# Where activation operands are rounded in a Strassen-staged layer, and two additions handed to accumulating DMAs

## The chip, the cores and the metric

One core of one Trainium2 chip runs the whole program. The metric is the device time of one execution in microseconds (us). Engines are called TensorE (PE in the rows, PEld for its weight loads), VectorE (DVE), ScalarE (ACT), GpSimd (POOL) and SyncE (SP, which here only issues DMAs).

## The reference, cut to what matters

The reference is one transformer-like layer for 640 token rows (512 of a prompt, 8 x 16 of a decode batch), with a model width of 2048. After the mixers (attention and a state-space group), which the change leaves alone, it computes

```python
h = x + merged @ w_out                                    # 2048 x 2048
f = rms_norm(h, g_ffn)
h = h + (silu(f @ w_gate) * (f @ w_up)) @ w_down          # 2048 x 5632, 5632 x 2048
gate = sigmoid(rms_norm(h, g_ple) @ w_ple_gate)           # 2048 x 2048
h = h + gate * (p_i @ w_ple_proj)
```

in float32. The three `h = ... + ...` are the additions that this document is about.

## The kernel before, in words

Features lie on the 128 partitions and the 640 tokens along the free axis. The five big products are done by one level of Strassen-Winograd: a tile of the output is 256 features x 640 tokens, held as `r` (128 x 2 x 640), and seven products of 128 x 320 each take the seven of the eight PSUM banks. The inner dimension goes in *units* of 512 rows. For each unit the `Ring` loads a 512 KB block of weights (`wst`, two buffers), VectorE makes four sums of its quadrants (`ws`, L109 to L112), ScalarE rounds quadrants and sums to a short format (`wh`, L86, once 128 x 768 from `wst` and once 128 x 1024 from `ws`) and VectorE takes what is left (`wl`, L87). The activations are held the same way as high and low parts in `kp` tiles of 2 x 7 x 320 (`cut`, L1050 on ScalarE and L1051 on VectorE; `whole` cuts all seven pieces). So each unit is 7 products x 2 halves x 3 = 42 matmuls of 128x128 on 128x320.

`strassen` runs a tile's units, then combines the seven banks into `r` (L1232 to L1240: two copies on ScalarE, six additions on VectorE, the last one, of `r12`, on GpSimd). The stages, in order:

- `o0` to `o7`: `w_out`, 4 units each, operand `km`. Then the residual `x` is added (L1280), the sum is scaled (`scaled`, L1267, ScalarE), the Winograd sums of its quadrants are written to `fc_dr`, `r` to `h_dr`, and its squares are added up (`squares`, L1249 to L1254: the square on ScalarE, the sums on VectorE).
- `g0`, `u0` to `g21`, `u21`: gate and up, 4 units each, operand `kf`, fetched from `fc_dr` during `o7`.
- `d0` to `d27`: the down product in 28 *cells* of 2 to 4 units (`down_cells`), operand `kt`. All but the last cell of each of the eight output tiles add their part to `h_dr` by an accumulating DMA from the GpSimd queue (L1346). The eight last cells (`d20` to `d27`, output tiles 4 to 7 and 0 to 3, 3 units each) add what `h_dr` holds (L1349, L1350), and go on as the `o` tiles do.
- `p0` to `p7`: the per-layer gate, 4 units each, operand `kh`. The gate is multiplied by a projection `pj`, then the running sum is loaded again (`hy`, L1372), added by GpSimd (L1373) and written out (L1374).

`pair` gives `r`, `x`, `hx`, `pj` and `hy` out of one pool with two buffers, `seven` the scaled tiles (one buffer). Each engine and each DMA queue works its instructions off in order, and that order is made by a scheduler that runs over the whole program when it is built: code that is written later in Python is not always later on the engine, and a moved call changes the order elsewhere. A second `x` tile is also the scratch for the squares.

Of the kernel before, what the change touches and what calls it, by code (L numbers as in the profile page):

```python
# [9 lines left out]
F32 = mybir.dt.float32  # L10
# [4 lines left out]
OP = mybir.AluOpType  # L15
# [4 lines left out]
P = 128  # L20
D = 2048
KT = D // P
NTOK = 640
# [141 lines left out]
def hybrid_step(ctx: ExitStack, tc: tile.TileContext, io):  # L165
    nc = tc.nc
# [5 lines left out]
    dp = ctx.enter_context(tc.tile_pool(reuse_waits="tile", name="dram", bufs=1, space=DRAM))  # L172
# [17 lines left out]
    ring = Ring(nc, stp, units)  # L190
# [4 lines left out]
    g_dr = dp.tile([1024, NTOK], F32, name="g_dr")  # L195
    m_dr = dp.tile([D, NTOK], F32, name="m_dr")
    h_dr = dp.tile([D, NTOK], F32, name="h_dr")
    h2_dr = dp.tile([D, NTOK], F32, name="h2_dr")
    tc_dr = dp.tile([FT // 2, P, 7, NH2], F32, name="tc_dr")
    fc_dr = dp.tile([KT // 2, P, 7, NH2], F32, name="fc_dr")  # L200
    hc_dr = dp.tile([KT // 2, P, 7, NH2], F32, name="hc_dr")
# [844 lines left out]
    def rows(dram, j):  # L1046
        return dram[2 * j * P : 2 * (j + 1) * P, :].rearrange("(a p) n -> p a n", p=P)
# [31 lines left out]
    for n in range(8):  # L1079
        ps = big(f"glu{n}")  # L1080
        g = gp_.tile([P, NTOK], F32, tag="xg", name=f"gre{n}", bufs=3)
# [61 lines left out]
    def pair(name):  # L1143
        return fo.tile([P, 2, NTOK], F32, tag="R", name=name, bufs=2)
# [12 lines left out]
    def kp_tile(name, i):  # L1157
        if i < 5:
            return kp_view(act_tile(name))
        if i == 5:  # L1160
            return fo.tile([P, 2, 7, NH2], F32R, tag="kp", name=name, bufs=1)
        return xp.tile([P, 2, 7, NH2], F32R, tag="kp", name=name, bufs=KB)

    def seven(name):
        return xp.tile([P, 7, NH2], F32, tag="c7", name=name, bufs=1)
# [6 lines left out]
    def whole(k, x):  # L1172
        cut(k, slice(0, 4), x[:, :4])
        cut(k, slice(4, 7), x[:, 4:])
        return k

    later = {}

    def fetch(name, slot, dram, i, late=False):
        k = kp_tile("k" + name, slot)  # L1180
        x = k[:, 1].bitcast(F32)
        nc.sync.dma_start(x, dram[i])
        if late:
            later.setdefault(i // 2 - 2, []).append(lambda: whole(k, x))
            return k
        return whole(k, x)

    def cut_late(u):
        for f in later.pop(u, ()):
            with tc.issue_after(ring.done[0]), tc.issue_after(ring.done[1]):  # L1190
                f()

    def products(name, kps, after=None, order=None):

        ps = {i: bank(f"{name}_{i}")[:, :NH2] for i in PRODUCTS}
        n = len(kps) // 2

        def product(i, u, cut):
            a, b = PRODUCTS[i]
            wh, wl = cut  # L1200
            for c in range(2):
                w = slice(c * P, (c + 1) * P)
                k = kps[2 * u + c]
                f, l = u == 0 and c == 0, u == n - 1 and c == 1
                nc.tensor.matmul(ps[i], wh[:, a, w], k[:, 0, b], start=f, stop=False)  # L1205
                nc.tensor.matmul(ps[i], wh[:, a, w], k[:, 1, b], start=False, stop=False)  # L1206
                nc.tensor.matmul(ps[i], wl[:, a, w], k[:, 0, b], start=False, stop=l)  # L1207

        for u in range(n if order is None else n - 2):
            cut = ring.next()  # L1210
            for i in PRODUCTS:
                product(i, u, cut)
            if after is not None:
                after(u)
        if order is not None:
            cuts = [ring.next() for _ in range(2)]
            for i in order:
                for u in range(2):
                    product(i, n - 2 + u, cuts[u])
        ring.ahead()  # L1220
        return ps
# [4 lines left out]
    def strassen(name, kps, after=None, into=None):  # L1226
        ps = products(name, kps, after)
        r = pair("r" + name) if into is None else into
        r11, r12, r21, r22 = blocks(r)
        q = fo.tile([P, NH2], F32, tag="q", name="q" + name, bufs=1)  # L1230
        tt = nc.vector.tensor_tensor
        nc.scalar.activation(q, ps[1], AF.Copy)  # L1232
        tt(r11, q, ps[2], op=OP.add)
        nc.scalar.activation(r12, ps[3], AF.Copy)
        tt(q, q, ps[6], op=OP.add)
        tt(r22, q, ps[7], op=OP.add)  # L1236
        tt(r12, r12, ps[5], op=OP.add)
        tt(r21, r22, ps[4], op=OP.subtract)
        tt(r22, r22, ps[5], op=OP.add)
        nc.gpsimd.tensor_tensor(r12, r12, q, op=OP.add)  # L1240
        return r
# [14 lines left out]
    def by_rows(x, s):  # L1256
        nc.vector.tensor_tensor(x, x, s[:, None, :].to_broadcast([P, 2, NTOK]), op=OP.mult)  # L1257
# [6 lines left out]
    def scaled(c, x, gain, j):  # L1264

        for a in range(2):
            nc.scalar.activation(c[:, 2 * a : 2 * a + 2], halves(x[:, a]), AF.Copy, scale=gain[:, 2 * j + a : 2 * j + a + 1])  # L1267

    fk = []
    for j in range(8):  # L1270
        after = None
        if j == 7:
            def after(u):
                for i in (2 * u, 2 * u + 1):
                    if i < 7:
                        fk.append(fetch(f"f{i}", i, fc_dr, i, late=i == 6))
        r = strassen(f"o{j}", mk, after)
        x = pair(f"x{j}")
        nc.sync.dma_start(x, io["xT"][2 * j : 2 * j + 2].rearrange("a p n -> p a n"))
        nc.vector.tensor_tensor(r, r, x, op=OP.add)  # L1280
        c = seven(f"c{j}")
        scaled(c, r, gffn, j)
        if j < 7:
            keep(nc.vector, c, fc_dr, j)
        else:
            winograd_rows(nc.vector, c[:, :4], c[:, 4:])
            kf7 = kp_tile("kf7", 7)
            fk.append(kf7)
            later.setdefault(1, []).append(lambda: whole(kf7, c))
        nc.sync.dma_start(rows(h_dr, j), r)  # L1290
        squares(ssqh, r, x, j == 0)

# [2 lines left out]
    def next_t():  # L1295

        u = len(tk) // 2
        if u < FT // 4:
            for i in (2 * u, 2 * u + 1):
                tk[i] = fetch(f"t{i}", slots[i % 8], tc_dr, i)  # L1300

    for f in range(FT // 2):
        z = strassen(f"g{f}", fk, cut_late if f == 0 else None)
        if f == 0:
            scale_rows(ssqh, D)
        by_rows(z, ssqh)
        nc.scalar.activation(z, z, AF.Silu)
        after = None
        if f == FT // 2 - 1:
            def after(u):  # L1310
                if u < 2:
                    next_t()
        c = seven(f"t{f}")
        t = c[:, :4].rearrange("p (a h) n -> p a (h n)", a=2)
        strassen(f"u{f}", fk, after, t)
        by_rows(t, ssqh)
        nc.vector.tensor_tensor(t, t, z, op=OP.mult)
        keep(nc.gpsimd, c, tc_dr, f)
# [12 lines left out]

    for n, (j, us, first, last) in enumerate(cells):
        def after(i, us=us, n=n):
            uses[us[i]] -= 1
            if not uses[us[i]] and n < len(cells) - 4:
                next_t()
            if n < 2 and i:
                next_t()
            if n == len(cells) - 1:
                for _ in range(min(2, 3 - i)):  # L1340
                    if ready:
                        next_h()

        r = strassen(f"d{n}", [tk[i] for u in us for i in (2 * u, 2 * u + 1)], after)
        if not last:
            nc.gpsimd.dma_start(rows(h_dr, j), r, accum_op=OP.add)  # L1346
            continue
        x = pair(f"hx{j}")
        nc.sync.dma_start(x, rows(h_dr, j))  # L1349
        nc.vector.tensor_tensor(r, r, x, op=OP.add)  # L1350
        c = seven(f"hc{j}")
        scaled(c, r, gple, j)
        if j in (3, 4, 5):
            winograd_rows(nc.vector, c[:, :4], c[:, 4:])
            hk[j] = whole(kp_tile(f"kh{j}", hslot[j]), c)
        else:
            keep(nc.vector, c, hc_dr, j)
            ready.append(j)
        nc.sync.dma_start(rows(h2_dr, j), r)
        squares(ssqp, r, x, j == 4)  # L1360
    hk = [hk[i] for i in (4, 5, 6, 7, 0, 1, 2, 3)]
    for j in range(7):
        z = strassen(f"p{j}", hk)
        if j == 0:
            scale_rows(ssqp, D)
        by_rows(z, ssqp)
        nc.scalar.activation(z, z, AF.Sigmoid)  # L1367
        x = pair(f"pj{j}")
        nc.sync.dma_start(x, rows(pj_dr, j))
        nc.vector.tensor_tensor(z, z, x, op=OP.mult)  # L1370
        x = pair(f"hy{j}")
        nc.sync.dma_start(x, rows(h2_dr, j))  # L1372
        nc.gpsimd.tensor_tensor(z, z, x, op=OP.add)  # L1373
        nc.sync.dma_start(rows(io["o_yT"], j), z)  # L1374


    x = pair("pj7")
    y = seven("hy7")[:, :4].rearrange("p (a h) n -> p a (h n)", a=2)
    nc.sync.dma_start(x, rows(pj_dr, 7))
    nc.sync.dma_start(y, rows(h2_dr, 7))  # L1380
    ps = products("p7", hk, order=(1, 2, 6, 5, 3, 7, 4))
    z = pair("rp7")
    r11, r12, r21, r22 = blocks(z)
# [143 lines left out]
```

## Time and profile before

| | |
|---|---|
| median of 3 runs | 2952.66 us (2950.65 to 2954.16) |
| the profiled execution | 2953.62 us, of which the span from first to last instruction is 2951.8 us |
| mean granted TensorE clock | 0.982 |
| busy share of the span: TensorE, VectorE, ScalarE, GpSimd | 96%, 77%, 42%, 14% |

The times of runs and of the profiled execution are of the same kind. The shares are means over stages that differ, so the rows below are taken stage by stage. In the rows, a name such as `ro` is the tile `r` of an `o` stage, `rd` of a `d` stage, `rp` of a `p` stage; buffer numbers are left out.

### The profile page before, as it was taken

Reading aid. Unit: us, or ns where it says so; the run is one execution under the profiler, and the core shown is the slowest. Engines: PE = TensorE matmul, PEld = TensorE weight load, DVE = VectorE, ACT = ScalarE, POOL = GpSimd, SP = SyncE. Lnnn points to the kernel's source line nnn. Section 1 sums busy time; section 2 is a strip of 40 time slices with the busy share of each in tenths; the row PEclk is TensorE's granted clock in tenths of the full one; section 3 lists DMA queues with packets and bytes.
Section 4 is the critical chain, followed back from the end, with each engine's and each line's share of the span. In section 5 each row is a group of like instructions: output and inputs, shape, how many; then the busy total and the mean of one; then the engine's idle time right before and its main releaser. Section 6 shows DMA issues by size and latency. Waiting matters only on the chain. (4 is left out here: it accounts for less than half of the span.)

```text
span 2951.8 us, 47685 instructions
## 1 busy us (share of the span) xinstructions
PE 2827.2 (96%) x19051; PEld 2717.0 (92%) x19051; DVE 2265.6 (77%) x3912; ACT 1240.9 (42%) x1627; POOL 420.7 (14%) x463
## 2 busy tenths in 40 slices
PE   8899999998799989999999999999999999999998
PEld 6789998887789889999999999999989999998898
DVE  8939354455698888787878787878886877899888
ACT  4333365555643453333333333333433444355433
POOL 6612310001000001010101010101020100100111
PEclk9999999999989999999999999999999999999999
DMA  5565744547534633233323333333554445647444
GB/s 168 153 180 159 224 168 173 176 145 260 191 133 172 223 139 123 100 116 101 118 100 118 101 117 102 117 102 117 190 159 139 144 158 175 164 153 271 139 156 143
DMA packets 137487, 449.19 MB, mean 152 GB/s; under 512 B 14096, under 2 KB 34672, under 8 KB 124464
## 3 DMA queue, kind: packets, MB, share of 16 engines
q1 hardware_dynamic: 120032, 396.47, 39.2%
q0 software_dynamic: 15936, 45.47, 6.2%
q10 hardware_dynamic: 1296, 4.20, 0.4%
q8 instruction: 149, 2.44, 0.3%
q14 instruction: 74, 0.61, 0.1%
HBM read 342.25 MB, written 101.18 MB: 150 GB/s over the span
## 5 line engine op out<-in xcount | busy, mean ns | idle before, releaser
L86 ACT ACTIVATE wh<-wst 128x768 fp32r<-128x768 f32 x328 | 276.9, 845 | 659.3 <-issue 319.9
L87 DVE TENSOR_TENSOR wl<-ws,wh 128x1024 fp32r<-128x1024 f32 x328 | 421.0, 1284 | 101.4 <-ACT wh L86 101.0
L86 ACT ACTIVATE wh<-ws 128x1024 fp32r<-128x1024 f32 x328 | 344.6, 1051 | 358.9 <-DVE ws L112 358.9
L87 DVE TENSOR_TENSOR wl<-wst,wh 128x768 fp32r<-128x768 f32 x328 | 337.5, 1029 | 169.3 <-ACT wh L86 169.3
L1205 PE MATMUL d<-kt,wh 128*128 128x320 f32 x1232 | 383.6, 315 | 11.8 <-ACT wh L86 5.1
L1205 PE MATMUL g<-kf,wh 128*128 128x320 f32 x1232 | 381.6, 310 | 5.5 <-ACT wh L86 5.4
L1206 PE MATMUL g<-kf,wh 128*128 128x320 f32 x1232 | 381.1, 310 | 0.0
L1205 PE MATMUL u<-kf,wh 128*128 128x320 f32 x1232 | 380.3, 309 | 0.5 <-DVE rg L1236 0.4
L1206 PE MATMUL d<-kt,wh 128*128 128x320 f32 x1232 | 380.7, 312 | 0.0
L1206 PE MATMUL u<-kf,wh 128*128 128x320 f32 x1232 | 380.1, 309 | 0.0
L1207 PE MATMUL g<-kf,wl 128*128 128x320 f32 x1232 | 375.6, 310 | 4.4 <-DVE wl L87 4.4
L1207 PE MATMUL u<-kf,wl 128*128 128x320 f32 x1232 | 376.1, 309 | 0.6 <-DVE wl L87 0.6
L1207 PE MATMUL d<-kt,wl 128*128 128x320 f32 x1232 | 344.5, 315 | 7.4 <-DVE wl L87 7.3
L1205 PEld LDWEIGHTS d<-kt,wh 128*128 128x128 f32 x1232 | 235.1, 191 | 17.7 <-ACT wh L86 9.7
L1205 PEld LDWEIGHTS g<-kf,wh 128*128 128x128 f32 x1232 | 232.1, 188 | 6.8 <-ACT wh L86 6.8
L1207 PEld LDWEIGHTS g<-kf,wl 128*128 128x128 f32 x1232 | 230.2, 188 | 5.5 <-DVE wl L87 5.2
L1206 PEld LDWEIGHTS d<-kt,wh 128*128 128x128 f32 x1232 | 235.1, 191 | 0.0
L1207 PEld LDWEIGHTS d<-kt,wl 128*128 128x128 f32 x1232 | 224.8, 191 | 11.2 <-DVE wl L87 10.6
L1206 PEld LDWEIGHTS g<-kf,wh 128*128 128x128 f32 x1232 | 232.2, 189 | 0.0
L1205 PEld LDWEIGHTS u<-kf,wh 128*128 128x128 f32 x1232 | 231.2, 188 | 1.0 <-DVE rg L1236 0.7
L1206 PEld LDWEIGHTS u<-kf,wh 128*128 128x128 f32 x1232 | 231.2, 188 | 0.0
L1207 PEld LDWEIGHTS u<-kf,wl 128*128 128x128 f32 x1232 | 230.0, 188 | 0.9 <-DVE wl L87 0.9
(499 smaller groups left out, 5981.2 us busy)
## 6 DMA issues: line engine op xcount, KB each, us to landing
wst<-in_w_gate SPq DMA_DIRECT2D x88, 512.0 KB
wst<-in_w_up SPq DMA_DIRECT2D x88, 512.0 KB
wst<-in_w_down SPq DMA_DIRECT2D x88, 512.0 KB
tc_dr<-t SPq DMA_DIRECT2D x22, 1120.0 KB
kt<-tc_dr SPq DMA_DIRECT2D x22, 1120.0 KB
wst<-in_w_qk SPq DMA_DIRECT2D x32, 512.0 KB
kc<-in_cache_k SPq DMA_DIRECT2D x16, 1024.0 KB
vc<-in_cache_v SPq DMA_DIRECT2D x16, 1024.0 KB
```

Source lines behind the costliest of these rows:

```text
L86: a = nc.scalar.activation(wh[:, part], x, AF.Copy)
L87: b = nc.vector.tensor_tensor(wl[:, part], x, wh[:, part].bitcast(F32), op=OP.subtract)
L1205: nc.tensor.matmul(ps[i], wh[:, a, w], k[:, 0, b], start=f, stop=False)
L1206: nc.tensor.matmul(ps[i], wh[:, a, w], k[:, 1, b], start=False, stop=False)
L1207: nc.tensor.matmul(ps[i], wl[:, a, w], k[:, 0, b], start=False, stop=l)
```

## The change

Three things are edited.

1. *Where operands are rounded.* `fetch` and the two places that called `whole` at once now put the cut into a list (`uncut`). `cut_next` takes the oldest entry of it; it is called after a unit's weights have been asked for, one or two entries at a time. `products` cuts what the coming unit still needs and has not been cut. `cut_late`, which tied two late cuts to the end of a unit's weights, goes.
2. *Residuals.* `residual` adds `x` (for `o0` to `o6`) and the running sum in `h_dr` (for `d20` to `d26`) to `r` by an accumulating DMA on the GpSimd queue, from HBM into `r`. The tile `x` stays as scratch for the squares. For `o7` and `d27` (`urgent`) the load and the VectorE addition stay.
3. *Final addition.* The last `d` cells write their sums to the output `o_yT` itself (only output tile 7 goes to a scratch, `h7_dr`), and the `p` tiles 0 to 6 are added to it by an accumulating DMA on the GpSimd queue; the load of `hy`, the GpSimd addition and the SyncE write go.

`squares` is not edited: its square stays on ScalarE, and its sums were on VectorE before.

```diff
-    h2_dr = dp.tile([D, NTOK], F32, name="h2_dr")
+    h7_dr = dp.tile([2 * P, NTOK], F32, name="h7_dr")
...
-    def fetch(name, slot, dram, i, late=False):
+    uncut = {}
+
+    def wait_cut(k, x):
+        uncut[id(k)] = lambda: whole(k, x)
+        return k
+
+    def fetch(name, slot, dram, i):
         k = kp_tile("k" + name, slot)
         x = k[:, 1].bitcast(F32)
         nc.sync.dma_start(x, dram[i])
...
-        return whole(k, x)
+        return wait_cut(k, x)
+
+    def cut_next(n=1):
+        for key in list(uncut)[:n]:
+            uncut.pop(key)()
...
             cut = ring.next()
+            for k in kps[2 * u : 2 * u + 2]:
+                if id(k) in uncut:
+                    uncut.pop(id(k))()
             for i in PRODUCTS:
                 product(i, u, cut)
...
+    def residual(r, src, name, urgent):
+        x = pair(name)
+        if urgent:
+            nc.sync.dma_start(x, src)
+            nc.vector.tensor_tensor(r, r, x, op=OP.add)
+        else:
+            nc.gpsimd.dma_start(r, src, accum_op=OP.add)
+        return x
...
-                        fk.append(fetch(f"f{i}", i, fc_dr, i, late=i == 6))
+                        fk.append(fetch(f"f{i}", i, fc_dr, i))
+                cut_next((0, 1, 2, 0)[u])
         r = strassen(f"o{j}", mk, after)
-        x = pair(f"x{j}")
-        nc.sync.dma_start(x, io["xT"][2 * j : 2 * j + 2].rearrange("a p n -> p a n"))
-        nc.vector.tensor_tensor(r, r, x, op=OP.add)
+        if j == 7:
+            cut_next()
+        x = residual(r, io["xT"][2 * j : 2 * j + 2].rearrange("a p n -> p a n"), f"x{j}", j == 7)
...
-        z = strassen(f"g{f}", fk, cut_late if f == 0 else None)
+        z = strassen(f"g{f}", fk, (lambda u: cut_next(2)) if f == 0 else None)
...
+                cut_next((0, 1, 1, 0)[u])
...
         strassen(f"u{f}", fk, after, t)
+        cut_next()
...
         def after(i, us=us, n=n):
+            cut_next()
...
-        x = pair(f"hx{j}")
-        nc.sync.dma_start(x, rows(h_dr, j))
-        nc.vector.tensor_tensor(r, r, x, op=OP.add)
+        x = residual(r, rows(h_dr, j), f"hx{j}", j == 3)
...
-            hk[j] = whole(kp_tile(f"kh{j}", hslot[j]), c)
+            hk[j] = wait_cut(kp_tile(f"kh{j}", hslot[j]), c)
...
-        nc.sync.dma_start(rows(h2_dr, j), r)
+        nc.sync.dma_start(rows(io["o_yT"] if j < 7 else h7_dr, j % 7), r)
...
-        z = strassen(f"p{j}", hk)
+        z = strassen(f"p{j}", hk, (lambda u: cut_next(2)) if j == 0 else None)
...
-        x = pair(f"hy{j}")
-        nc.sync.dma_start(x, rows(h2_dr, j))
-        nc.gpsimd.tensor_tensor(z, z, x, op=OP.add)
-        nc.sync.dma_start(rows(io["o_yT"], j), z)
+        nc.gpsimd.dma_start(rows(io["o_yT"], j), z, accum_op=OP.add)
```

Below are three places of the order. Numbers behind `wh`, `ws` and `wst` count units through the program, and lines of the change stand four higher (L1271 is the line that was L1267, L1253 that was L1249).

ScalarE between the copies out of tile `o2` and those out of `o3` (whose units are 96 to 99), before:

```order
L1234 ACTIVATE ro2_8939<-o2_3_8714 128x320
L86 ACTIVATE wh96_8871<-ws96_8873 128x1024
L86 ACTIVATE wh97_8926<-wst97_8827 128x768
L1267 ACTIVATE c2_8953<-ro2_8939,c_g_ffn_134 128x640 x2
L1249 ACTIVATE x2_8950<-ro2_8939 128x1280
L86 ACTIVATE wh98_9014<-wst98_8882 128x768
L86 ACTIVATE wh97_8926<-ws97_8928 128x1024
L86 ACTIVATE wh98_9014<-ws98_9016 128x1024
L86 ACTIVATE wh99_9069<-wst99_8937 128x768
```

and with the change:

```order
L1238 ACTIVATE ro2_8937<-o2_3_8712 128x320
L86 ACTIVATE wh96_8869<-ws96_8871 128x1024
L86 ACTIVATE wh97_8924<-wst97_8825 128x768
L86 ACTIVATE wh97_8924<-ws97_8926 128x1024
L86 ACTIVATE wh98_9011<-wst98_8880 128x768
L1271 ACTIVATE c2_8950<-ro2_8937,c_g_ffn_134 128x640 x2
L1253 ACTIVATE x2_8948<-ro2_8937 128x1280
L86 ACTIVATE wh98_9011<-ws98_9013 128x1024
L86 ACTIVATE wh99_9066<-wst99_8935 128x768
```

The scaling and the square of `r` have moved behind two more roundings of weights; what stands right behind them is now the 128 x 1024 part of unit 98, and before it was unit 98's 128 x 768 part and unit 97's 128 x 1024 part.

ScalarE behind the copies out of cell `d22` (the units of `d23` are 365 to 367), before:

```order
L1234 ACTIVATE rd22_25565<-d22_3_25393 128x320
L86 ACTIVATE wh365_25497<-ws365_25499 128x1024
L86 ACTIVATE wh366_25552<-wst366_25453 128x768
L86 ACTIVATE wh367_25640<-wst367_25508 128x768
L1267 ACTIVATE hc6_25579<-rd22_25565,c_g_ple_136 128x640 x2
L1249 ACTIVATE hx6_25576<-rd22_25565 128x1280
L86 ACTIVATE wh366_25552<-ws366_25554 128x1024
```

and with the change:

```order
L1238 ACTIVATE rd22_25556<-d22_3_25382 128x320
L86 ACTIVATE wh366_25543<-wst366_25444 128x768
L86 ACTIVATE wh365_25488<-ws365_25490 128x1024
L86 ACTIVATE wh366_25543<-ws366_25545 128x1024
L1271 ACTIVATE hc6_25569<-rd22_25556,c_g_ple_136 128x640 x2
L1253 ACTIVATE hx6_25567<-rd22_25556 128x1280
L86 ACTIVATE wh367_25630<-wst367_25499 128x768
```

Here the first part of the third unit, 367, has moved from ahead of the scaling to behind it.

VectorE at the same place, before (`hc6` is the scaled tile, whose sums L118 to L121 wait for the scaling):

```order
L112 TENSOR_TENSOR ws366_25554<-wst366_25453,ws366_25554 128x256
L87 TENSOR_TENSOR wl367_25641<-wst367_25508,wh367_25640 128x768
L118 TENSOR_TENSOR hc6_25579<-hc6_25579 128x320
L119 TENSOR_TENSOR hc6_25579<-hc6_25579 128x320
L120 TENSOR_TENSOR hc6_25579<-hc6_25579 128x320
L121 TENSOR_TENSOR hc6_25579<-hc6_25579 128x320
L1253 TENSOR_TENSOR ssq_105<-ssq_105,hx6_25576 128x640
L87 TENSOR_TENSOR wl366_25553<-ws366_25554,wh366_25552 128x1024
```

and with the change:

```order
L87 TENSOR_TENSOR wl366_25544<-ws366_25545,wh366_25543 128x1024
L118 TENSOR_TENSOR hc6_25569<-hc6_25569 128x320
L109 TENSOR_TENSOR ws367_25632<-wst367_25499 128x256
L110 TENSOR_TENSOR ws367_25632<-wst367_25499 128x256
L119 TENSOR_TENSOR hc6_25569<-hc6_25569 128x320
L120 TENSOR_TENSOR hc6_25569<-hc6_25569 128x320
L111 TENSOR_TENSOR ws367_25632<-ws367_25632,wst367_25499 128x256
L1257 TENSOR_TENSOR ssq_105<-ssq_105,hx6_25567 128x640
L121 TENSOR_TENSOR hc6_25569<-hc6_25569 128x320
L87 TENSOR_TENSOR wl367_25631<-wst367_25499,wh367_25630 128x768
```

The sums of the scaled tile have moved behind the last part of unit 366; the weight sums of unit 367 and its `wl` now stand among and behind them.

SyncE's queue in the last cell `d27`, where the operands of `p0` are fetched (`rd26` is the tile of the cell ahead), before:

```order
L1182 DMA kh6_26432<-hc_dr_77 128x2240
L1182 DMA kh7_26438<-hc_dr_77 128x2240
L1359 DMA h2_dr_74<-rd26_26357 128x2x640
```

and with the change:

```order
L1373 DMA o_yT<-rd26_26344 128x2x640
L1187 DMA kh6_26418<-hc_dr_77 128x2240
L1187 DMA kh7_26420<-hc_dr_77 128x2240
L1187 DMA kh0_26481<-hc_dr_77 128x2240
L1187 DMA kh1_26483<-hc_dr_77 128x2240
```

The write of `rd26`, which needs the finished sum, now stands ahead of the four loads.

## Rows read from the trace of the kernel before

**Rows 1.** Page, parts 1 and 5: engine, busy; line, operation, count, mean ns.

```profile
PE 2827.2 (96%) x19051; PEld 2717.0 (92%) x19051; DVE 2265.6 (77%) x3912; ACT 1240.9 (42%) x1627; POOL 420.7 (14%) x463
L86 ACT ACTIVATE wh<-ws 128x1024 fp32r<-128x1024 f32 x328 | 344.6, 1051 | 358.9 <-DVE ws L112 358.9
```

**Rows 2.** ScalarE in order of time, gate and up stages: start, duration, operation.

```profile
1418.53 0.42 ACT L1232 ACTIVATE qg<-g 128x320 f32<-128x320 f32 x1
1443.17 0.42 ACT L1232 ACTIVATE qu<-u 128x320 f32<-128x320 f32 x1
```

**Rows 3.** Windows (PE, PEld, DVE, ACT, POOL busy; clock; DMA), two stretches.

```profile
1005.00:1100.00 95.00, 79.64 (x501) 75.47 (x501) 83.70 (x126) 53.31 (x59) 2.61 (x3) 0.96 0.49 184
2556.00:2699.00 143.00, 136.31 (x897) 131.17 (x896) 130.99 (x217) 68.38 (x84) 8.32 (x8) 1.00 0.56 183
```

**Rows 4.** ScalarE in order of time, one `o` tile; in brackets the idle time ahead.

```profile
896.58 0.42 ACT L1232 ACTIVATE qo<-o 128x320 f32<-128x320 f32 x1
...
907.82 1.55 ACT L1267 ACTIVATE c<-ro,c_g_ffn 128x640 f32<-128x640 f32 x2 [5.28 <-DVE ro L1280]
909.28 1.26 ACT L1249 ACTIVATE x<-ro 128x1280 f32<-128x1280 f32 x1
...
922.91 0.41 ACT L1232 ACTIVATE qo<-o 128x320 f32<-128x320 f32 x1
```

**Rows 5.** ScalarE in order of time, first and last of eight `d` cells.

```profile
2556.23 0.44 ACT L1234 ACTIVATE rd<-d 128x320 f32<-128x320 f32 x1 [3.26 <-PE d L1207]
...
2698.65 0.44 ACT L1234 ACTIVATE rd<-d 128x320 f32<-128x320 f32 x1 [3.36 <-issue]
```

**Rows 6.** ScalarE in order of time, two `p` tiles.

```profile
2785.49 0.42 ACT L1232 ACTIVATE qp<-p 128x320 f32<-128x320 f32 x1
...
2811.07 0.42 ACT L1232 ACTIVATE qp<-p 128x320 f32<-128x320 f32 x1
```

**Rows 7.** One line's instructions, L1346: durations in ns; landing in us from issue.

```profile
L1346 POOL DMA_DIRECT2D h_dr<-rd x20: 1195/1204/1305, 2168.9 to 2562.9; - x20
...
DMA to landing us min/median/max: 6.6/8.0/14.0
```

**Rows 8.** DMA issues: tile, queue, count, KB each, median us to landing.

```profile
db<-d_dr POOLq DMA_DIRECT2D x8, 512.0 KB, 5.2
```

**Rows 9.** VectorE in order of time, a `d` cell's last addition into `rd`.

```profile
2549.55 0.47 DVE L1239 TENSOR_TENSOR rd<-rd,d 128x320 f32<-128x320 f32 x1
```

**Rows 10.** GpSimd in order of time, the accumulating DMA of that cell.

```profile
2550.56 1.20 POOL L1346 DMA_DIRECT2D h_dr<-rd  x1 [2.41 <-DVE ws L111]
```

**Rows 11.** VectorE in order of time, the `o` tile of rows 4.

```profile
901.87 0.49 DVE L1237 TENSOR_TENSOR ro<-ro,o 128x320 f32<-128x320 f32 x1 [0.16 <-PE o L1207]
...
905.24 0.47 DVE L1239 TENSOR_TENSOR ro<-ro,o 128x320 f32<-128x320 f32 x1
```

**Rows 12.** VectorE in order of time, one of the last `d` cells (`d21`).

```profile
2599.85 0.49 DVE L1237 TENSOR_TENSOR rd<-rd,d 128x320 f32<-128x320 f32 x1 [0.17 <-ACT wh L86]
...
2602.36 0.47 DVE L1239 TENSOR_TENSOR rd<-rd,d 128x320 f32<-128x320 f32 x1
...
2606.14 0.42 DVE L112 TENSOR_TENSOR ws<-wst,ws 128x256 f32<-128x256 f32 x1
...
2607.35 0.49 DVE L118 TENSOR_TENSOR hc<-hc 128x320 f32<-128x320 f32 x1
...
2609.28 0.82 DVE L1253 TENSOR_TENSOR ssq<-ssq,hx 128x640 f32<-128x640 f32 x1
```

**Rows 13.** GpSimd in order of time, the addition of one `p` tile.

```profile
2803.29 3.77 POOL L1373 TENSOR_TENSOR rp<-rp,hy 128x1280 f32<-128x1280 f32 x1 [10.59 <-DMA hy<-h_dr]
```

**Rows 14.** VectorE in order of time, a rounding during that addition, and the next.

```profile
2804.47 3.40 DVE L87 TENSOR_TENSOR wl<-wst,wh 128x768 fp32r<-128x768 f32 x1 [0.24 <-ACT wh L86]
...
2811.60 0.95 DVE L87 TENSOR_TENSOR wl<-wst,wh 128x768 fp32r<-128x768 f32 x1
```

**Rows 15.** SyncE's queue in order of time: the load of `kh6` and `kh7`.

```profile
2705.19 0.80 SPq L1182 DMA_DIRECT2D kh<-hc_dr x2
```

More of the change, by code (lines that the diff above doesn't have):

```diff
@@ L1175, in whole @@
         return k
-    later = {}
-    def fetch(name, slot, dram, i, late=False):
+    uncut = {}
[3 more added lines that the diff above has]
+    def fetch(name, slot, dram, i):
         k = kp_tile("k" + name, slot)
@@ L1182, in fetch @@
         nc.sync.dma_start(x, dram[i])
-        if late:
-            later.setdefault(i // 2 - 2, []).append(lambda: whole(k, x))
-            return k
-        return whole(k, x)
[L1188 to L1191, printed above, removed]
+        return wait_cut(k, x)
+    def cut_next(n=1):
+        for key in list(uncut)[:n]:
+            uncut.pop(key)()
     def products(name, kps, after=None, order=None):
@@ L1286, in hybrid_step @@
             winograd_rows(nc.vector, c[:, :4], c[:, 4:])
-            kf7 = kp_tile("kf7", 7)
-            fk.append(kf7)
-            later.setdefault(1, []).append(lambda: whole(kf7, c))
+            fk.append(wait_cut(kp_tile("kf7", 7), c))
         nc.sync.dma_start(rows(h_dr, j), r)
@@ L1379, in hybrid_step @@
     nc.sync.dma_start(x, rows(pj_dr, 7))
-    nc.sync.dma_start(y, rows(h2_dr, 7))
+    nc.sync.dma_start(y, rows(h7_dr, 0))
     ps = products("p7", hk, order=(1, 2, 6, 5, 3, 7, 4))
```

## Prediction

> **What bounds the kernel now.** I read the page first: TensorE is busy for 96% of the span, VectorE for 77%, GpSimd for 14% [rows 1]. So the end is set by TensorE, and an edit gains or loses only what TensorE stands still. The next view is ScalarE in order of time where the gate and up products run: the same copy at a tile's end comes 24.64 us after the one before [rows 2]. A tile of four units is 4 x 42 = 168 matmuls, so one takes 24.64 / 168 = 0.1467 us and a unit 6.16 us. That is the full rate, and the measure for the other stages; gate and up have nothing to give back. Then the windows [rows 3], whose matmul counts times 0.1467 us show what is lost: between 1005 and 1100 us (the change from `o7` to `g0`) 95 - 501 x 0.1467 = 21.5 us, with VectorE busy for 83.7 of the 95; in the last `d` cells 143 - 897 x 0.1467 = 11.4 us, with VectorE busy for 131 of the 143. The time lines say it by tile: an `o` tile takes 922.91 - 896.58 = 26.33 us [rows 4], 1.69 over the full rate; a last `d` cell (2698.65 - 2556.23) / 7 = 20.35 us [rows 5], 1.87 over its three units (18.48); a `p` tile 25.58 us [rows 6], 0.94 over. These losses and the transitions are what the change touches.
>
> **What the accumulating DMA costs.** No DMA of the kernel before adds into on-chip memory. The nearest row is L1346, the same queue, size and adding with HBM as the target: 20 issues of 1.2 us each, landing 6.6 us after the issue at best, 8.0 at the median, 14.0 at worst [rows 7]. The other near row is a plain load on the same queue, 512 KB in 5.2 us [rows 8], which by size is 5.2 x 640 / 512 = 6.5 us. I take 7.5, between the two and nearer to the one that adds, with bounds of 6.5 and 14. L1346 starts 0.54 us behind the last VectorE addition, 2550.56 - (2549.55 + 0.47) [rows 9, 10]. So 8.0 us go by from the finished `r` to the finished sum.
>
> The Trainium skill, "DMA: Bandwidth & Descriptors", section "Latency and other measured facts", puts most of a DMA's fixed cost on the round trip to the target memory, HBM being the slowest target. By that rule these DMAs would land earlier than L1346's; no row of before shows it.
>
> **`o0` to `o6`.** Removed: the VectorE addition L1280, behind which ScalarE stood idle for 5.28 us [rows 4]. Added: the landing. In tile `o2` the last bank is read at 901.87, and the last addition ends at 905.24 + 0.47 = 905.7 [rows 11]; with its roundings ahead it may be some 0.4 earlier in the new order, 905.3. The sum is there at 913.3, the scaling (1.55 for both) done at 914.8, the square (1.26) at 916.1 [rows 4], and the 128 x 1024 rounding of unit 98 (1.05 [rows 1]), which the order shows right behind it, at 917.1. TensorE takes that rounding after units 96 and 97 and the three products of unit 98 that use plain quadrants: 42 + 42 + 18 = 102 matmuls or 15.0 us behind the tile's end at 901.7, at 916.7. It stands for 0.4 us; `wl` from the same sums, on VectorE behind the sums of the scaled tile, adds perhaps 0.2. The present loss of 1.69 goes, because the two roundings that stood behind the scaling now precede it. (0.6 - 1.69) x 7 = **-8 us**. Bounds: a landing at 6.5 gives -1.69 x 7 = -12; at 9.0, +0.4 x 7 = +3.
>
> **`d20` to `d26`.** Here the third unit is wanted already after two units, less the matmuls by which TensorE is in the next cell when the last bank is read: four, so 80 x 0.1467 = 11.7 us. The order has two kinds of cell. In three of them (`d20`, `d22`, `d24`) VectorE does all sums of the third unit among and behind those of the scaled tile, as shown for `d22`. There `r` is finished some 3.4 us behind the last bank read (2.98 now [rows 12], and one weight rounding more ahead), the sum at 11.4, the scaling done at 12.9. Behind it stand four sums of the scaled tile (0.49 each), three weight sums (0.42), one square sum (0.82) [rows 12] and `wl` (0.95 [rows 14]), 5.0 us by their lengths and about 4.4 as they overlap by some 0.08 each: 17.3. TensorE wants this `wl` six matmuls into the unit, at 12.6, so it stands for 4.7 us, 2.8 more than now. In the other four the weight sums of the third unit are ahead; there only its second `wl` waits, behind the scaled tile's sums, the square sums and an addition of the next cell, and TensorE stands for about 2.0, as now. 3 x 2.8 + 4 x 0.1 = **+9 us**. Bounds: a landing at 6.5 gives +2, at 9.0 +20. The VectorE addition saved is within these sums.
>
> **The cuts.** In `o7` to `g0` VectorE is busy for 83.7 of 95 us [rows 3], and both kernels give it the same cuts. Placing them one by one can win at most its idle time, 11.3 us, if that is all due to order; it wins nothing if the rounding work itself is the limit. Nearer to the second: **-1 us**, bounds -11 and +3. Elsewhere the cuts keep their place on the path: 0.
>
> **`d27` to `p0`.** The loads of `kh6` and `kh7` go out at 2705.19 [rows 15]. On SyncE's queue they now stand behind the write of `rd26`, which waits for its landing. Late next are these loads, by up to 6.5 us, then the cuts, then `kh0` and `kh1`, which stand in the same queue. `p0` takes `kh6` and `kh7` only in a later unit, which covers most: **+2 us**, bounds 0 and +6.
>
> **`p0` to `p6`.** GpSimd's addition takes 3.77 us [rows 13], and a VectorE rounding beside it takes 3.40 where the next takes 0.95 [rows 14]. Addition, load and write go; in their place stand one POOL issue of 1.2 us and a DMA for which no engine waits, since the buffer of `rp` is next written a tile (24.6 us) later. Of the 0.94 lost per tile I take nearly all back: **-6 us**; bounds -6.6 and 0 (if the loss has another cause).
>
> **Sum.** -8 + 9 - 1 + 2 - 6 = -4 us on the profiled 2953.6, which lies 1 us above the median; in terms of the median 2949 us. A measurement of this kernel can tell about 0.2%, 5.9 us, from no change, so this is within it.
>
> `squares` is not edited, so the part of the description that speaks of squares on VectorE moves nothing: the square stays on ScalarE (L1253 in the order).
>
> **Rivals.**
> *A, the forecast*: 2949, its own range 2941 to 2960. Chance 0.45.
> *B, the landing is quick*, 6.5 us or sooner: -4 more in `o` and -7 in `d`, 2938. For it: the plain load [rows 8], and 6.6 occurs [rows 7]. Against: the median of L1346. Chance 0.22.
> *C, slower: the landing is late.* In the last cells the DMA engines are busy for 0.56 of the time, at 183 GB/s [rows 3], and 14.0 us occurs [rows 7]. Once TensorE stands, each microsecond of landing costs one in each of the 14 tiles, for ScalarE waits at the scaling and VectorE at its sums, with the third unit behind both. At 9.0 us: 2949 + 1.5 x 14 = 2970. It makes the change slower from a landing of about 8.2 us, since (2952.7 + 5.9 - 2949) / 14 = 0.7. Against: most of the 20 landings are at 8 or below. Chance 0.25.
> The Trainium skill, "SBUF — State Buffer", names in its "DVE blocks DMA" trap a mechanism for C: GpSimd cannot write a DMA's descriptors while VectorE runs certain copies. The 20 issues at 1195 to 1305 ns [rows 7] show no such delay.
> *D, the placed cuts help*: VectorE's idle 11.3 us at `g0` are due to order, and 10 us more come back: 2940. For it: a late cut holds up all sums behind it. Against: VectorE is nearly full there. Chance 0.08.
>
> **From these to the numbers.** Faster: all of B, three quarters of D (0.06) and 0.12 of A, whose forecast lies 3.7 us below the median: 0.40. Slower: all of C and 0.05 of A: 0.30. Same: the rest, 0.30. The range reaches from beyond B to beyond C at 9.0: 2930 to 2976.
>
> **What would show it.** *Landing*: the new POOL issues land 7 to 8 us after the issue; 6.5 is B, over 8.2 is C. *o*: the tile period falls to about 25.2. *d*: the cell period rises to about 21.6, TensorE waiting for `wl` from VectorE, and VectorE idle ahead of L118 for the scaling; the cells `d20`, `d22`, `d24` are the long ones. *Cuts*: 1005 to 1100 holds about as many matmuls as now. *p0*: the `kh6` load is issued several us later against the end of `d26`. *p*: the period falls to 24.6 to 24.9 and no VectorE rounding is stretched. The prediction is wrong first of all if the landing is not near 7.5 us, as 14 tiles hang on it; then if VectorE or ScalarE is not held as the order has it.

## The result, and the profile after

The changed kernel takes 2984.14 us (median of 4 runs, 2982.59 to 2989.81) against 2951.9 us for the kernel before (4 runs here, so not quite the median of 3 above); the ratio is 1.0108, 95% interval 1.0095 to 1.012. It is 32 us slower where 3 us faster was forecast, and 8 us beyond the upper end of the forecast range. The profiled execution took 2983.43 us, span 2981.7 us, granted clock 0.976 (0.982 before).

The page of the changed kernel, part 1 and the end of part 4 (shares of the span on the chain that ended last, by line):

```profile
PE 2844.5 (95%) x19051; PEld 2735.1 (92%) x19051; DVE 2230.0 (75%) x3898; ACT 1241.0 (42%) x1627; POOL 419.8 (14%) x477
PE u L1208 6%; PE u L1206 6%; PE u L1207 6%; PE g L1206 6%; PE g L1207 6%; PE g L1208 6%; PE d L1208 5%; PE d L1206 4%; PE d L1207 4%; PE p L1206 2%; PE p L1208 2%; PE p L1207 2%; DVE wl L87 2%; DMA rd<-h_dr 1%; DMA ro<-in_xT 1%
```

VectorE has 36 us less work than in [rows 1], and the residual DMAs of both stages now stand on the chain, with 1% each. TensorE does the same 19051 matmuls but is busy for 17 us *longer*: some of them ran more slowly.

Where the time went is read by following one copy per tile through both traces. The first copy out of `o1` starts 0.2 us later than before; that of `o7` 18.05 us later; the second copy (L1234, now L1238) of `d19` 15.9 us later, that of `d26` 30.3; the first copy of `p1` 34.1 us later, that of `p6` 30.0, and the end 29.9. So the `o` stage lost 18 us, the stretch from `o7` to `d19` gave back 2, `d20` to `d26` lost 14.4, the way into `p1` another 3.8, and `p1` to `p6` gave back 4.1.

One `o` tile of the changed kernel, ScalarE in order of time; it answers to [rows 4]:

```profile
900.12 0.42 ACT L1236 ACTIVATE qo<-o 128x320 f32<-128x320 f32 x1
...
917.71 1.55 ACT L1271 ACTIVATE c<-ro,c_g_ffn 128x640 f32<-128x640 f32 x2 [5.47 <-DMA ro<-in_xT]
919.17 1.25 ACT L1253 ACTIVATE x<-ro 128x1280 f32<-128x1280 f32 x1
920.33 1.04 ACT L86 ACTIVATE wh<-ws 128x1024 fp32r<-128x1024 f32 x1
...
927.62 0.42 ACT L1236 ACTIVATE qo<-o 128x320 f32<-128x320 f32 x1
```

VectorE and GpSimd in the same tile:

```profile
904.86 1.22 DVE L87 TENSOR_TENSOR wl<-ws,wh 128x1024 fp32r<-128x1024 f32 x1
906.00 0.48 DVE L1241 TENSOR_TENSOR ro<-ro,o 128x320 f32<-128x320 f32 x1
...
908.23 0.41 DVE L109 TENSOR_TENSOR ws<-wst 128x256 f32<-128x256 f32 x1
908.57 0.41 DVE L110 TENSOR_TENSOR ws<-wst 128x256 f32<-128x256 f32 x1
908.90 0.47 DVE L1243 TENSOR_TENSOR ro<-ro,o 128x320 f32<-128x320 f32 x1
...
918.57 0.49 DVE L118 TENSOR_TENSOR c<-c 128x320 f32<-128x320 f32 x1 [4.18 <-ACT c L1271]
```

```profile
909.91 1.19 POOL L1280 DMA_DIRECT2D ro<-in_xT  x1 [2.42 <-issue]
```

The sum lands 917.71 - 909.91 = 7.8 us after its issue, the scaling starts at once, and the rounding behind scaling and square ends at 921.37. TensorE in order of time, the stall of the tile before and of this one:

```profile
893.24 0.41 PE L1206 MATMUL o<-km,wh 128*128 128x320 f32 x1 [3.06 <-ACT wh L86]
...
921.42 0.42 PE L1206 MATMUL o<-km,wh 128*128 128x320 f32 x1 [1.76 <-ACT wh L86]
```

Both wait for exactly the rounding that the forecast named. What follows them differs. Windows of 2 us in the same stretch (TensorE busy, matmuls, granted clock, DMA share, GB/s):

```profile
888.00:890.00 2.00, 2.00 (x15) 1.00 0.18 33
890.00:892.00 2.00, 0.17 (x2) 1.00 0.79 278
892.00:894.00 2.00, 0.76 (x4) 0.95 1.08 372
894.00:896.00 2.00, 2.00 (x9) 0.50 1.01 428
896.00:898.00 2.00, 2.00 (x12) 0.70 0.22 90
...
920.00:922.00 2.00, 0.58 (x4) 1.00 0.92 261
922.00:924.00 2.00, 2.00 (x14) 1.00 0.90 376
```

After the wait of 1.76 us TensorE goes on at full clock; after that of 3.06 us the granted clock is 0.50, the 1.2 GHz level, and matmuls come 0.27 us apart instead of 0.15 for some 3 us. That second price was not in the forecast.

The landings of all 14 residual DMAs, and their issues:

```profile
L1280 POOL DMA_DIRECT2D ro<-in_xT x7: 1180/1187/1302, 857.5 to 1022.1; - x7
L1280 POOL DMA_DIRECT2D rd<-h_dr x7: 1189/1199/1212, 2597.2 to 2736.4; - x7
...
DMA to landing us min/median/max: 6.3/7.7/12.4
```

The worst one is `o6`. GpSimd, SyncE and ScalarE there:

```profile
1022.13 1.19 POOL L1280 DMA_DIRECT2D ro<-in_xT  x1 [2.43 <-issue]
...
1034.58 1.55 ACT L1271 ACTIVATE c<-ro,c_g_ffn 128x640 f32<-128x640 f32 x2 [9.83 <-DMA ro<-in_xT]
```

```profile
1023.55 0.88 SPq L1187 DMA_DIRECT2D kf<-fc_dr  x2
```

Two operand loads of 1120 KB each go out 1.4 us behind it. That they delay the landing is likely, but no run parts the two: every run that left the whole of `o6`'s addition to one DMA had such loads close behind it, and landed after 12.4 to 13.5 us. TensorE then stands for 6.1 us and runs at half clock behind that.

The last `d` cells, ScalarE at the ends of `d19` and `d26` (this answers to [rows 5], seven cells), and the late landing of `d23` on TensorE:

```profile
2572.14 0.44 ACT L1238 ACTIVATE rd<-d 128x320 f32<-128x320 f32 x1 [3.25 <-PE d L1208]
...
2728.91 0.44 ACT L1238 ACTIVATE rd<-d 128x320 f32<-128x320 f32 x1 [3.72 <-issue]
```

```profile
2678.39 0.41 PE L1206 MATMUL d<-kt,wh 128*128 128x320 f32 x1 [4.55 <-ACT wh L86]
```

That is 156.77 / 7 = 22.40 us per cell, 2.05 over [rows 5]. ScalarE and VectorE behind `d23`, where the last weight sum of the third unit (L112) stands behind the scaled tile's L118, and the rounding that needs it (2677.29) behind the scaling:

```profile
2674.36 1.55 ACT L1271 ACTIVATE hc<-rd,c_g_ple 128x640 f32<-128x640 f32 x2 [7.05 <-issue]
...
2677.29 1.04 ACT L86 ACTIVATE wh<-ws 128x1024 fp32r<-128x1024 f32 x1
```

```profile
2675.22 0.49 DVE L118 TENSOR_TENSOR hc<-hc 128x320 f32<-128x320 f32 x1 [5.52 <-ACT hc L1271]
2675.63 0.42 DVE L112 TENSOR_TENSOR ws<-wst,ws 128x256 f32<-128x256 f32 x1
```

VectorE behind `d20`:

```profile
2596.17 0.47 DVE L1243 TENSOR_TENSOR rd<-rd,d 128x320 f32<-128x320 f32 x1
...
2604.47 0.49 DVE L118 TENSOR_TENSOR hc<-hc 128x320 f32<-128x320 f32 x1 [2.75 <-ACT hc L1271]
...
2607.82 0.95 DVE L87 TENSOR_TENSOR wl<-wst,wh 128x768 fp32r<-128x768 f32 x1
```

From L118 to the end of the third unit's `wl` it takes 4.3 us (4.4 forecast). TensorE waits first for ScalarE's rounding of that unit and then for this `wl`:

```profile
2607.10 0.42 PE L1206 MATMUL d<-kt,wh 128*128 128x320 f32 x1 [0.91 <-ACT wh L86]
...
2608.83 0.41 PE L1208 MATMUL d<-kt,wl 128*128 128x320 f32 x1 [0.58 <-DVE wl L87]
```

Two `p` tiles, ScalarE, as in [rows 6]; the period is 24.84 us, down from 25.58:

```profile
2844.43 0.42 ACT L1236 ACTIVATE qp<-p 128x320 f32<-128x320 f32 x1
2869.27 0.42 ACT L1236 ACTIVATE qp<-p 128x320 f32<-128x320 f32 x1
```

### The profile page after: what moved, and what is told of

The parts are those of the page before. It is cut to its first block, busy times and chain, and to the rows that moved or that the text cites. A ratio compares the mean times of both kernels' runs of the same rounds, so it can differ in the third digit from the quotient of the medians.

```text
span 2981.7 us, 47652 instructions
## 1 busy us (share of the span) xinstructions
PE 2844.5 (95%) x19051; PEld 2735.1 (92%) x19051; DVE 2230.0 (75%) x3898; ACT 1241.0 (42%) x1627; POOL 419.8 (14%) x477
## 4 chain that ended last, share of the span: by engine, by line
PE 57%; DVE 7%; DMA 4%; issue 4%; ACT 2%; DVEq 0%; SPq 0%; ACTq 0%; POOLq 0%
PE u L1208 6%; PE u L1206 6%; PE u L1207 6%; PE g L1206 6%; PE g L1207 6%; PE g L1208 6%; PE d L1208 5%; PE d L1206 4%; PE d L1207 4%; PE p L1206 2%; PE p L1208 2%; PE p L1207 2%; DVE wl L87 2%; DMA rd<-h_dr 1%; DMA ro<-in_xT 1%
## 5 line engine op out<-in xcount | busy, mean ns | idle before, releaser
L87 DVE TENSOR_TENSOR wl<-ws,wh 128x1024 fp32r<-128x1024 f32 x328 | 406.1, 1238 | 105.4 <-ACT wh L86 104.8
```

What stands on the lines that cost most here:

```text
L87: b = nc.vector.tensor_tensor(wl[:, part], x, wh[:, part].bitcast(F32), op=OP.subtract)
```

## The experiments

The theory was that the residual DMAs cost the time: ScalarE and VectorE wait, in order, for the landing, the weight work of the third unit stands behind them, and after a long stall TensorE runs at the lower clock for a while. The rivals: the placed cuts spoil the order, or the added DMA traffic does it wherever the wait stands. Each time is a median over runs, the ratio is to the kernel before on the same chips.

**All residuals back on VectorE** (cuts and final DMA stay).

```diff
-        if urgent:
+        if True:
```

> The changed kernel with every residual loaded by SyncE and added by VectorE, as before; the placed cuts and the accumulating final addition stay. Theory (the residual DMAs: ScalarE and VectorE wait in order for the landing, with the weight work of the third unit behind them, and TensorE runs at the lower clock after a long stall): the 17 us lost in the o stage and the 24 us lost in the last d cells come back, 2984 - 41 = 2943, between 2938 and 2948. Rival (the new places of the cuts make the order worse, and the residuals are innocent): the kernel stays at 2975 or above.

Measured: 2948.92 us, ratio 0.9991 (0.9981 to 1.0). About 35 us come back. That is 1 us above the stated range, and far from the rival: the cuts are innocent. `o1` to `o6` takes 131.5 us again, as before.

**Residual DMAs alone**, in the kernel before.

```diff
-        nc.sync.dma_start(x, rows(h_dr, j))
-        nc.vector.tensor_tensor(r, r, x, op=OP.add)
+        nc.gpsimd.dma_start(r, rows(h_dr, j), accum_op=OP.add)      # j != 3; likewise o0 to o6
```

> The kernel before with the 14 residual additions made by accumulating DMAs, and nothing else. Theory (residual DMAs): about 41 us slower than before, 2985 to 2997, with the stalls at the same places as in the changed kernel (third unit's wh from ScalarE) and stretches of half clock behind those over 2.5 us. Rival (the cuts): within 6 us of 2952.

Measured: 2989.15 us, ratio 1.013 (1.0113 to 1.0146), 37 us slower: the whole loss, and a little more, is in this one edit. The landings take 7.9 us (`o`) and 6.6 us (`d`) at the median. One of its stalls on TensorE:

```profile
978.00 0.63 PE L1205 MATMUL o<-km,wh 128*128 128x320 f32 x1 [3.28 <-ACT wh L86]
```

**Final addition alone**, in the kernel before.

```diff
-        nc.sync.dma_start(x, rows(h2_dr, j))
-        nc.gpsimd.tensor_tensor(z, z, x, op=OP.add)
-        nc.sync.dma_start(rows(io["o_yT"], j), z)
+        nc.gpsimd.dma_start(rows(io["o_yT"], j), z, accum_op=OP.add)   # the last d cells write to o_yT, as in the change
```

> The kernel before with the final addition made by accumulating DMAs into the output, and nothing else. Theory: the p tiles lose no time to GpSimd's addition any more, 5 us faster, 2945 to 2949, tile period of the p stage about 24.8 us. Rival (the gain in the p stage comes from the placed cuts or another source): within 2 us of 2952.

Measured: 2948.61 us, ratio 0.9987 (0.9978 to 0.9996), 3 us faster. This kernel and the one with all residuals on VectorE (2948.92 us) differ in the cuts alone, so the cuts neither cost nor bring anything that these runs can tell. The tile period of the `p` stage is the changed kernel's:

```profile
2835.65 0.42 ACT L1232 ACTIVATE qp<-p 128x320 f32<-128x320 f32 x1
2860.49 0.42 ACT L1232 ACTIVATE qp<-p 128x320 f32<-128x320 f32 x1
```

**Only the `o` residuals back on VectorE.**

```diff
-        x = residual(r, ..., f"x{j}", j == 7)
+        x = residual(r, ..., f"x{j}", True)
```

> The changed kernel with the residuals of o0 to o6 on VectorE and those of d20 to d26 left as accumulating DMAs. Theory: the o stage gives back its 17 us and the d cells keep their loss: 2964 to 2970. Rival (one common cause, such as DMA traffic of the added queue, or an order spoilt everywhere): a gain under 8 us, 2976 or above.

Measured: 2966.51 us, ratio 1.0055 (1.0041 to 1.0069). 18 us come back in the `o` stage, and of the 14.4 us lost from `d19` to `d26` 11.6 stay: the two losses are of the same kind, and each stands without the other.

**The scaling held behind the third unit.**

```diff
+    def follow():
+        if todo:
+            f = todo.pop()
+            with tc.issue_after(ring.done[0]), tc.issue_after(ring.done[1]):
+                f()          # scaled, keep, the write of r, squares of the tile before
...
+            if u == 1:
+                follow()     # from the next tile's units; also in the d cells
```

> The changed kernel, accumulating residual DMAs and all, but the scaling, the sums, the write and the squares of a tile are held until the weights of the third unit of the next tile have been rounded. Theory (what costs is not the landing by itself but the weight work queued behind it): the stalls at the third unit go in both stages, the o tiles fall to about 24.7 us, and the time to 2935 to 2948, some 41 us less than the changed kernel. Rival (the landing costs wherever the wait stands, since the fourth unit, or the buffer of r, or the first unit of the next cell is late instead): 2965 or above.

Measured: 2963.64 us, ratio 1.003 (1.0021 to 1.0039): a miss for the size, and under the rival's bound as well. The `o` tiles did what the theory says, with the landing as long as ever (median 7.9 us, both stages): `o1` to `o6` takes 125.7 us, 25.1 a tile, 5.8 us less than before for the five. The same DMAs move the same bytes here, so it was not their traffic that slowed the `o` tiles. But `o6` to `o7` stays at 33.1 us, since its landing is later than even the held place, and now the fourth unit waits:

```profile
1016.85 1.06 ACT L86 ACTIVATE wh<-ws 128x1024 fp32r<-128x1024 f32 x1 [2.15 <-DVE ws L112]
1026.51 1.55 ACT L1271 ACTIVATE c<-ro,c_g_ffn 128x640 f32<-128x640 f32 x2 [8.61 <-DMA ro<-in_xT]
```

And from `d20` to `p1` it takes 224.7 us, 9 less than the changed kernel and 13 more than with VectorE. A cell of three units has no fourth to cover the held work. Two copies there also waited for the write of `r` to leave its buffer (1.9 us together); how the rest divides was not settled.

**Each residual DMA in two halves.**

```diff
-            nc.gpsimd.dma_start(r, src, accum_op=OP.add)
+            for a in range(2):
+                nc.gpsimd.dma_start(r[:, a], src[:, a], accum_op=OP.add)
```

> The changed kernel with each residual DMA cut in two of half the size, 320 KB each. Theory one (bytes and a second issue on GpSimd's queue decide: the second half lands no sooner than the whole did): within 8 us of the changed kernel, 2976 to 2992. Theory two (a fixed part that overlaps decides less than size, so both halves land some 2 us sooner): 14 tiles lose 2 us less each and their stretches of half clock go, 2940 to 2960.

Measured: 2956.02 us, ratio 1.0009 (1.0 to 1.0018). Theory two: 28 us come back. A half lands sooner:

```profile
ro<-in_xT POOLq DMA_DIRECT2D x14, 320.0 KB, 5.4
...
rd<-h_dr POOLq DMA_DIRECT2D x14, 320.0 KB, 4.8
```

It is not the landing alone: the first half is issued before the last addition into `r`, the scaling of that half moves ahead of a rounding of the third unit in ScalarE's order, and `r` is finished earlier. The run does not part these.

**The `o` tiles held, the `d` residuals on VectorE.**

```diff
-        x = residual(r, rows(h_dr, j), f"hx{j}", j == 3)
+        x = residual(r, rows(h_dr, j), f"hx{j}", True)      # and the held scaling, in o only
```

> As the run with the scaling held back, for the o tiles alone; d20 to d26 add their residual on VectorE as before. Theory: the o tiles lose neither the 1.69 us of before nor the new stalls, 2934 to 2942, 10 us under the run with all residuals on VectorE. Rival (the held scaling makes another unit late): 2947 or above.

Measured: 2946.76 us, ratio 0.9976 (0.9966 to 0.9986): 5 us above the theory's range and at the bound of the rival, with both sides partly right. `o1` to `o6` takes 127.3 us, 4.2 less than before, and `o6` to `o7` takes 31.9, some 7 more than with VectorE.

**The combination.**

```diff
-        x = residual(r, ..., f"x{j}", j == 7)
+        x = residual(r, ..., f"x{j}", j >= 6)      # o0 to o5: two halves, scaling held
```

> The combination that the runs point to: o0 to o5 add x by two accumulating DMAs of 320 KB each and hold the scaling until the third unit of the next tile is rounded; o6, o7 and the d cells add on VectorE; placed cuts and accumulating final addition as in the changed kernel. Theory (the o tiles lose neither the old 1.5 us stall nor a new one, and the long tile o6 to o7 of the held run, 32 us, falls back to 25): 2938 to 2944, 6 us or more under the 2949 with all residuals on VectorE. Rival (the o stalls are only moved into other tiles): 2946 to 2950.

Measured: 2941.97 us, ratio 0.9963 (0.995 to 0.9977), 11 us faster than before and the fastest of all. ScalarE, one `o` tile:

```profile
897.43 0.44 ACT L1236 ACTIVATE qo<-o 128x320 f32<-128x320 f32 x1 [0.72 <-PE o L1208]
...
912.27 1.06 ACT L86 ACTIVATE wh<-ws 128x1024 fp32r<-128x1024 f32 x1 [2.65 <-DVE ws L112]
913.23 1.58 ACT L1271 ACTIVATE c<-ro,c_g_ffn 128x640 f32<-128x640 f32 x2
...
922.07 0.44 ACT L1236 ACTIVATE qo<-o 128x320 f32<-128x320 f32 x1 [0.86 <-PE o L1208]
```

The period is 24.64 us, the full rate of [rows 2]. The third unit's rounding precedes the scaling, and the scaling has no idle time ahead of it: the DMA has landed by then. Neither the held scaling nor the halves do this alone: from `o1` to `o6` the held scaling takes 125.7 us, the two halves 128.6, both together 123.3.

**Four quarters.**

```diff
-                nc.gpsimd.dma_start(r[:, a], src[:, a], accum_op=OP.add)
+                for b in range(2):
+                    h = slice(b * NH2, (b + 1) * NH2)
+                    nc.gpsimd.dma_start(r[:, a, h], src[:, a, h], accum_op=OP.add)
```

> The changed kernel with each residual DMA cut in four of 160 KB. Theory one (the last piece lands when GpSimd has issued all four in a row, so there is nothing more to win after two): 2952 to 2962, as with two pieces. Theory two (each halving of the size brings the landing nearer): 2948 or below.

Measured: 2948.14 us, ratio 0.9981 (0.9972 to 0.999), 0.14 above the bound of theory two, and clearly under theory one. A quarter lands after 4.5 (`o`) and 4.2 us (`d`), only some 0.8 us sooner than a half; but the quarters follow the additions into `r` one by one. Behind the copy at 898.57 the first is issued at 901.88, 6.5 us ahead of the end of the last addition at 908.43:

```profile
901.88 0.84 POOL L1283 DMA_DIRECT2D ro<-in_xT  x1 [17.04 <-DVE ro L1237]
...
907.99 1.72 POOL L1283 DMA_DIRECT2D ro<-in_xT  x2 [0.67 <-DVE ro L1242]
```

Stretches by the starts of the first copies (`o1`, `o6`, `o7`, `d20`, `p1`, `p6`) and of the second copy out of `d26` in each trace, us:

```
                        o1-o6   o6-o7   d20-p1   d26-p1   p1-p6
before                  131.5    25.9    215.1     86.8   128.3
changed                 141.8    33.5    233.8     90.7   124.2
residuals on VectorE    131.5    25.0    211.8     83.5   124.0
residual DMA alone      141.8    33.8    233.9     93.4   127.9
final addition alone    131.5    26.2    212.7     83.3   124.0
o residual on VectorE   131.5    25.4    228.5     88.5   124.0
scaling held            125.7    33.1    224.7     94.1   124.0
two halves              128.6    28.7    216.7     85.3   124.0
o held, d on VectorE    127.3    31.9    212.7     83.6   124.5
combination             123.3    25.1    211.8     83.5   124.0
four quarters           124.6    29.8    214.6     84.4   124.0
```

The start of `o1` itself differs by up to 5.8 us between the traces, so stretches are compared here and not totals.

## Why the prediction was wrong, point by point

**The mechanism was right in kind.** ScalarE waits at the scaling, VectorE at the sums of the scaled tile, and TensorE at the third unit's weights, as forecast; in the `d` cells most of the loss stands in other cells than forecast. The residual DMA alone carries the loss.

**The landing, 7.5 us, and the start 0.54 us behind the last addition: right.** 7.7 us at the median, and 909.91 - (908.90 + 0.47) = 0.54. Rival C, a late landing at large, is not what happened: the change is slower although the median landing is as forecast. The rule of the Trainium skill, "DMA: Bandwidth & Descriptors", section "Latency and other measured facts", by which a target other than HBM should answer sooner, shows faintly at most: 7.7 us into on-chip memory (7.9 in `o`, 6.8 in `d`) against 8.0 into HBM [rows 7], in different stages.

**`o0` to `o6`, -8 us: the step that failed first; it cost 18.** Three things were mis-sized. First, "it may be some 0.4 earlier in the new order" was the wrong way round. Two weight sums (L109 and L110) now stand ahead of the last addition into `r`, at 908.23 and 908.57; before, they stood behind it (it starts at 905.24 [rows 11]):

```profile
905.63 0.41 DVE L109 TENSOR_TENSOR ws<-wst 128x256 f32<-128x256 f32 x1
905.97 0.41 DVE L110 TENSOR_TENSOR ws<-wst 128x256 f32<-128x256 f32 x1
```

Taking the 1.83 us between the second copy and the last bank read of [rows 11] (901.87 - 900.04, the start of L1234 in the trace of before), the tile that ended with the copy at 903.27 was ready to be read at 905.1; `r` was finished at 909.37, 4.3 us later, against 3.84 before and 3.4 assumed. With 0.3 us more of landing the sum came 12.6 us behind the tile's end, not 11.4, and that turns the forecast stall of 0.4 into the 1.76 seen. Second, the median stood for all landings. By the scaling's start, the seven took 6.6, 8.6, 7.8, 8.1, 7.8, 8.0 and 12.4 us; a tile that gains nothing below 7 us and loses all above is priced by the spread, and `o6` alone cost 7.6 us. Third, "once TensorE stands, each microsecond of landing costs one" left out the clock. Adding up the gaps between matmul starts over 0.1467 us from `o1` to `o7`, stalls (gaps over 0.5 us) rose from 9.9 to 18.6 us, and what came at about half rate behind them from 1.3 to 9.2 us: nearly half of the loss.

**`d20` to `d26`, +9 us: right in sign, 14.4 measured, but in other cells; this step failed too.** The stretches behind `d20`, `d22` and `d24`, called the long ones, took 22.5, 24.0 and 23.5 us against 21.3, 21.4 and 21.0 before, 6.4 us more in all where 8.4 was forecast. Behind `d20` the VectorE chain was right to 0.1 us, but it began earlier (the landing took 6.4 us, not 7.5), and TensorE stood for 0.91 + 0.58 us, not 4.7. Behind `d21`, `d23` and `d25`, where no more than now was forecast, it took 20.4, 23.7 and 22.8 us against 22.3, 18.0 and 18.0: 10.5 us were lost in the last two. The forecast had only a second `wl` wait there, and a stall of about 2.0 us already there. But before, these two stretches took no longer than the full rate of 18.48. With the change ScalarE's 128 x 1024 rounding of the third unit stands behind the scaling in both (behind `d23` VectorE's last weight sum waits for the scaling too), so it waits for the landing as well, 8.8 and 7.2 us, and not only the `wl` made from it. TensorE stood for 4.55 and 3.18 us at that rounding, with the lower clock on top as in the `o` stage.

**The cuts, -1 us: no gain is shown.** From `o7` to `d19` 2.1 us came back (1528.4 to 1526.3), but not by the cuts: with the cuts and all residuals on VectorE this stretch takes 1528.3 us, and with the residual DMAs and without the cuts 1525.6.

**`d27` to `p0`, +2 us: right in place, too small.** The way into `p1` became 3.8 us longer, but two edits meet in it: the residual DMAs alone make it 6.6 us longer, the final addition alone 3.6 shorter (`d26-p1` in the table). So the term was nearer to 7, above its bound of 6. SyncE's queue shows the four loads held behind the write, as forecast; the first goes out 16.4 us behind the copy out of `d26`, where it was 6.5 [rows 5, 15], so it is late by 9.8 us and not by 6.5:

```profile
2744.84 0.40 SPq L1373 DMA_DIRECT2D o_yT<-rd  x1
2745.29 2.77 SPq L1187 DMA_DIRECT2D kh<-hc_dr  x4
```

**The final addition, -6 us: right.** 4.1 us over the five tiles from `p1` to `p6`, 0.81 a tile of the 0.94, and some 3 more on the way into `p1` (3.6 alone, 2.7 beside the residual DMAs). Alone it brought 3 us at the median (1 to 6 by its interval).

So -4 became +30 in the profiled executions mainly because 18 + 14.4 stood where -8 + 9 was forecast: `r` was finished later than assumed, the spread of the landings was left out, the third unit's rounding behind `d23` and `d25` was taken to be free of the landing, and the loss of a stall was taken as the stall alone.

## What to carry to other kernels

Replacing an addition by an accumulating DMA trades 1.5 us of VectorE for some 8 us of latency; in these runs it cost nothing only where no work that was wanted sooner stood behind its reader on an in-order queue. Hold the reader behind that work, cut the DMA into pieces that follow the pieces of the result, and leave on the engine the tiles whose DMA goes out beside large loads. When a stall is priced, look at the granted clock behind stalls of that length in the same kernel, and price the spread of a latency, not its median.

## What the runs showed of the hardware

Stalls are counted here as the gap between two matmul starts less 0.1467 us, which is some 0.15 more than the idle time that the rows show in brackets. Lone stalls of TensorE of 1.5 to 1.6 us in the `o` stage (some 25 in the traces here) left the clock as it was and cost 0.1 to 0.2 us more; the eleven of 2.8 us and over between `o1` and `o7` (up to 7.8 us) were followed by stretches at the 1.2 GHz level that cost 1 to 2.9 us on top. In between, one of 1.94 us cost 1.6 more, another of 1.91 us 0.2. The length of one stall alone does not decide: in the last `d` cells one of 1.4 us (final addition alone) was followed by a granted clock of 0.50 and 1.7 us of loss, and one of 3.3 us (two halves) by a clock of 1.00 and 0.1 us. The Trainium skill, "TensorE: Matmul & The Clock Gate", Part 1, says that an idle engine falls to half rate and must work its way back; the granted clock of 0.50 behind the 3.06 us wait agrees, that of 1.00 behind the stall of 3.3 us does not show it.

An accumulating DMA into on-chip memory took 7.7 us at the median for 640 KB, about 5 for 320 KB and 4.2 to 4.5 for 160 KB, at 1.2 us of GpSimd per issue for the whole and 0.85 for a part.
